# Wide projections with tokens on partitions, and small products issued by chunk halves in turn, in a two-layer hybrid decoder trunk

## The chip, the cores and the metric

The kernel runs on one core of a Trainium2 chip (trn2). The metric is the device time of one execution in microseconds, where lower is better. Three runs of the kernel before took 1239.12, 1239.46 and 1240.7 us, so the median is 1239.46 us.

## The reference

The reference computes DEPTH = 2 decoder layers on 256 tokens of 1024 features, in fp32. Cut to what matters here, one layer is:

```python
proj = x @ w_in                      # columns: q/kv ranks, DeltaNet q k v, HGRN2 q f i, output gates, 3 x 1024 branch gates
a = mla_branch(...)                  # 256 x 512, latent attention
b = gated_deltanet_branch(...)       # 256 x 512, chunks of 64 tokens, triangular solve, scan over 4 chunks
c = hgrn2_branch(...)                # 256 x 512, chunks of 64 tokens, scan over 4 chunks
merged = sum(sigmoid(gate_i) * (branch_i @ w_br_i))      # three branches, each projected to 1024
x = layer_norm(alpha * x + merged @ w_out)
x = layer_norm(alpha * x + moe(x))   # top-1 of 4 groups, top-2 of its 8 SwiGLU experts of width 256
```

The w_in, w_br and w_out products are dense: 256 tokens against 1024 or 512 rows. The chunked branches make many small products of 64 tokens by 64 tokens, or 64 by 128, per head (4 heads) and per chunk (4 chunks of 64 tokens).

## The kernel before

**Stages of a layer.** `layer` (L549) runs the mixer stages in a fixed order of code: decay, latent attention, DeltaNet keys, triangular inverse (`dn_inverse`, L775), queries, values, HGRN2 projections (`hg_project`, L929), HGRN2 local attention (`hg_local`, L951), the two scans (`dn_scan` L872, `hg_scan` L1020), the merge of branch a, the output gates (`gates`, L1051), the merge of branches b and c, `project_out` (L1233), and then the mixture of experts (`moe`, L1453). The framework orders each engine's instructions by readiness in a simulated run, with code order as priority, so dense products of later stages fill the gaps of the earlier ones on TensorE; on the chip every engine then runs its own list in order.

**Dense products.** Weights come in chunks of 1 MB (256 columns by 1024 rows for w_in and w_out; 512 by 512 for the branch projections) into four rotating buffers by DMAs on SP's queue, and from the second half of the mixer on also into 12, then 4 more, prefetch buffers for the experts (`open_prefetch`, L200). Each chunk is split in two pieces of 1024 elements per partition: ScalarE writes the rounded high part `wh` (L225) and VectorE the remainder `wl` (L226; four named pieces go to GpSimd). `mm3` (L234) then makes three fp32r matmuls per 128x128 block: high by high (L237), and the two cross terms (L238, L239). `dense_cm` (L241) holds 128 weight columns stationary and moves 256 tokens, so features land on partitions; `dense_tm` (L252) holds 128 tokens stationary and moves 256 weight columns. Both move 256 columns per matmul. Their results alternate between two PSUM banks, `ps_pa` and `ps_po`: a chunk's 48 matmuls fill one bank, while the other is being read.

**Merge.** For each 256 features of a branch, `merge_branch` (L1213) makes the gate chunk (L1219, `dense_cm`), a tanh by ScalarE (L1221), the branch projection (24 matmuls), the product by VectorE (L1229) and for b and c the addition by GpSimd (L1231) into `mixT`, which has features on partitions. `project_out` splits `mixT` into high and low parts (L1237) and multiplies with w_out in four chunks; after each, `route` (L1243) transposes the new residual and feeds the router product (L1254).

**Small products.** They are plain fp32, each shown as two matmul instructions. `key_products` (L763) and `pairs` (L980) hold 64 tokens (64 output partitions, K = 128): all heads of chunk half 0, then all of half 1. `prod` (L791) and `flip` (L798, L800) in `dn_inverse` work on 64x64 blocks (K = 64, 64 output partitions), half 0 first, then half 1; `flip` uses transposes for half 0 and products with the identity for half 1. `hg_scan` issues, per chunk and head, the product with the state (L1032, K = 128) and the local product (L1033, K = 64) by turns, and after them the state's update (L1038, K = 64, 128 output partitions).

## Time and profile before

| | |
|---|---|
| median of 3 runs | 1239.46 us (1239.12 to 1240.7) |
| the profiled execution | 1233.71 us, span 1231.9 us |
| PE (TensorE matmul) busy | 1090.1 us, 88% |
| PEld (weight load) busy | 842.8 us, 68% |
| DVE / ACT / POOL busy | 639.2 / 439.9 / 181.4 us |
| granted TensorE clock, mean | 0.953 |
| bytes moved | 305.68 MB, mean 248 GB/s |

A matmul's row shows its whole passage through the array, so consecutive matmuls overlap and a busy PE is not a PE at its peak: the distance from one start to the next is the cost of a matmul in a stream, and a merged row of n matmuls spans n - 1 distances plus one passage. A wait that is shorter than a passage doesn't show as idle time.

### The profile page before, as it was taken

Reading aid. Unit: us, or ns where it says so; the run is one execution under the profiler, and the core shown is the slowest. Engines: PE = TensorE matmul, PEld = TensorE weight load, DVE = VectorE, ACT = ScalarE, POOL = GpSimd, SP = SyncE. Lnnn points to the kernel's source line nnn. Section 1 sums busy time; section 2 is a strip of 40 time slices with the busy share of each in tenths; the row PEclk is TensorE's granted clock in tenths of the full one; section 3 lists DMA queues with packets and bytes.
Section 4 is the critical chain, followed back from the end, with each engine's and each line's share of the span. In section 5 each row is a group of like instructions: output and inputs, shape, how many; then the busy total and the mean of one; then the engine's idle time right before and its main releaser. Section 6 shows DMA issues by size and latency. Waiting matters only on the chain. (4 is left out here: it accounts for less than half of the span.)

```text
span 1231.9 us, 23305 instructions
## 1 busy us (share of the span) xinstructions
PE 1090.1 (88%) x9772; PEld 842.8 (68%) x9772; DVE 639.2 (52%) x1320; ACT 439.9 (36%) x812; POOL 181.4 (15%) x168
## 2 busy tenths in 40 slices
PE   6999999999998998777789999899999988977774
PEld 4788987899995644333378889869999944533332
DVE  7775766376567522111086766844766592311113
ACT  4654553354444211000067436535443341100001
POOL 2400033000111400000023010610011141000001
PEclk9999999999999999788899999999999999978887
DMA  8721340358966699999993214205598559999995
GB/s 222 212 70 36 115 150 11 103 172 280 388 247 247 267 419 421 420 422 420 397 243 112 69 37 142 99 1 172 184 355 355 200 228 421 420 422 421 421 420 185
DMA packets 127817, 305.68 MB, mean 248 GB/s; under 512 B 21027, under 2 KB 93149, under 8 KB 102365
## 3 DMA queue, kind: packets, MB, share of 16 engines
q1 hardware_dynamic: 127708, 304.15, 66.6%
q8 instruction: 78, 1.28, 0.4%
q14 instruction: 31, 0.25, 0.1%
HBM read 303.08 MB, written 1.05 MB: 247 GB/s over the span
## 5 line engine op out<-in xcount | busy, mean ns | idle before, releaser
L226 DVE TENSOR_TENSOR wl<-w,wh 128x1024 fp32r<-128x1024 f32 x150 | 203.5, 1358 | 108.3 <-ACT wh L225 108.1
L1550 PE MATMUL ps_pa<-w,xg 128*32 128x256 f32 x2304 | 193.1, 450 | 75.0 <-DMA w<-in_exp_w_up_dram 40.7
L225 ACT CAST wh<-w 128x1024 fp32r<-128x1024 f32 x158 | 165.3, 1047 | 205.5 <-PE ps_pa L238 84.4
L1550 PEld LDWEIGHTS ps_pa<-w,xg 128*32 128x32 f32 x2304 | 89.6, 128 | 174.9 <-DMA w<-in_exp_w_up_dram 54.0
L1557 DVE SCALAR_TENSOR_TENSOR hm<-ps_pa,ws,hm 128x256 f32<-128x256 f32 x18 | 8.7, 484 | 229.8 <-ACT hm L1556 229.8
L237 PE MATMUL ps_pa<-hTh,wh 128*128 128x256 f32 (+1 forms) x360 | 103.3, 287 | 1.9 <-ACT wh L626 1.9
L239 PE MATMUL ps_po<-hTh,wl 128*128 128x256 f32 (+1 forms) x360 | 103.8, 288 | 1.2 <-DVE wl L226 1.2
L239 PE MATMUL ps_pa<-hTh,wl 128*128 128x256 f32 (+1 forms) x360 | 103.2, 287 | 1.5 <-DVE wl L226 1.3
L237 PE MATMUL ps_po<-hTh,wh 128*128 128x256 f32 (+1 forms) x360 | 103.9, 289 | 0.0
L238 PE MATMUL ps_pa<-hTl,wh 128*128 128x256 f32 (+1 forms) x360 | 102.7, 285 | 0.0
L238 PE MATMUL ps_po<-hTl,wh 128*128 128x256 f32 (+1 forms) x360 | 102.5, 285 | 0.0
L1556 ACT ACTIVATE hm<-ps_pa 128x256 f32<-128x256 f32 x18 | 6.9, 384 | 254.1 <-PE ps_pa L1550 254.1
L1576 PE MATMUL ps_pm<-w,hmT 128*32 128x512 f32 x576 | 79.4, 597 | 4.4 <-ACT xg L1504 2.8
L239 PEld LDWEIGHTS ps_pa<-hTh,wl 128*128 128x128 f32 (+1 forms) x360 | 67.4, 187 | 3.7 <-DVE wl L226 2.7
L237 PEld LDWEIGHTS ps_pa<-hTh,wh 128*128 128x128 f32 (+1 forms) x360 | 67.6, 188 | 3.3 <-ACT wh L626 2.1
L239 PEld LDWEIGHTS ps_po<-hTh,wl 128*128 128x128 f32 (+1 forms) x360 | 67.2, 187 | 3.3 <-DVE wl L226 2.7
L237 PEld LDWEIGHTS ps_po<-hTh,wh 128*128 128x128 f32 (+1 forms) x360 | 67.6, 188 | 1.6 <-issue 0.9
L238 PEld LDWEIGHTS ps_po<-hTl,wh 128*128 128x128 f32 (+1 forms) x360 | 67.5, 187 | 0.8 <-issue 0.2
L238 PEld LDWEIGHTS ps_pa<-hTl,wh 128*128 128x128 f32 (+1 forms) x360 | 67.4, 187 | 0.5
L231 DVE TENSOR_TENSOR Yl<-ps_pm,Yh 128x512 fp32r<-128x512 f32 x36 | 24.8, 690 | 72.2 <-ACT Yh L230 65.1
L1576 PEld LDWEIGHTS ps_pm<-w,hmT 128*32 128x32 f32 x576 | 21.0, 109 | 51.0 <-issue 34.7
L226 POOL TENSOR_TENSOR wl<-w,wh 128x1024 fp32r<-128x1024 f32 x8 | 19.5, 2448 | 189.1 <-ACT wh L225 189.1
(486 smaller groups left out, 2460.9 us busy)
## 6 DMA issues: line engine op xcount, KB each, us to landing
w<-in_exp_w_gate_dram SPq DMA_DIRECT2D x66, 1024.0 KB
w<-in_exp_w_up_dram SPq DMA_DIRECT2D x66, 1024.0 KB
w<-in_exp_w_down_dram SPq DMA_DIRECT2D x66, 1024.0 KB
w<-in_w_in_dram SPq DMA_DIRECT2D x58, 1024.0 KB
w<-in_w_out_dram SPq DMA_DIRECT2D x8, 1024.0 KB
w<-in_w_br_a_dram SPq DMA_DIRECT2D x4, 1024.0 KB
w<-in_w_br_b_dram SPq DMA_DIRECT2D x4, 1024.0 KB
w<-in_w_br_c_dram SPq DMA_DIRECT2D x4, 1024.0 KB
```

The costliest lines, as they stand in the source:

```text
L225: nc.scalar.copy(v(hi), raw)
L226: engine.tensor_tensor(v(lo), raw, v(hi).bitcast(F32), op=OP.subtract)
L231: (engine or self.nc.vector).tensor_tensor(lo, src, hi.bitcast(F32), op=OP.subtract)
L237: mm(ps, a[0], b[0], start=start, stop=False, skip_group_check=True)
L238: mm(ps, a[0], b[1], start=False, stop=False, skip_group_check=True)
L239: mm(ps, a[1], b[0], start=False, stop=stop, skip_group_check=True)
L1550: nc.tensor.matmul(pg[32 * e:32 * e + 32, FF * n:FF * n + FF], xgs[gp, k // 4][j][:, k % 4, 32 * e:32 * e + 32], w[:, FF * k:FF * k + FF], ...
L1556: nc.scalar.activation(hm, pg[:, 0:FF], AF.Silu)
L1557: self.last_hm = nc.vector.scalar_tensor_tensor(hm, pg[:, FF:2 * FF], PTs[gp][1][:, j], hm, op0=OP.mult, op1=OP.mult).ins
L1576: nc.tensor.matmul(ps[32 * e:32 * e + 32], hmT[:, i, 32 * e:32 * e + 32], w[:, D * i + 512 * c:D * i + 512 * c + 512], start=(i == 0), sto ...
```

## The change

- The columns of HGRN2's i, of the two output gates, of the three branch gates and of w_out come in chunks of 512 columns by 512 rows (two chunks make one output of 512 features). They and the branch projections go through a new `dense_tm`: 128 tokens stationary, 512 weight columns moving, so that tokens lie on partitions. One output of 512 features now fills both banks, one per token block of 128, and each piece is used first for block 0 (6 matmuls), then for block 1 (6).
- `merge_branch` works on 512 features at a time, with two tanh, two products and two additions into `mix` (tokens on partitions).
- `mix` is transposed on TensorE (`mix_turned`) in two halves: the first before the last branch projection, the second after the first half of w_out's first output. The split into high and low reads PSUM then.
- `project_out` makes two outputs of 512 features; `route` works per token block and 512 features.
- `key_products`, `prod`, `flip` and `pairs` issue the two chunk halves in turn, head by head; `flip` uses products with the identity for both.
- `hg_scan` issues the state's updates of both halves in turn, then all local products of both halves in turn, and then those with the state.
- The pool `sg` has 4 buffers where it had 3.

The core of the diff:

```diff
-    def dense_tm(self, ps, raw, act, name):
-
-        nk = raw.shape[1]
-        for k0 in range(0, nk, 4):
-            w = self.split(raw[:, k0:k0 + 4], f"{name}.{k0 // 4}")
+    def dense_tm(self, ps, raw, act, name, k0, nk):
+
+
+        for j in range(0, 4, 2):
+            w = self.split(raw[:, j:j + 2], f"{name}.{j // 2}")
             for t in range(TB):
-                for k in range(4):
-                    self.mm3(ps[t], [x[:, k0 + k, 128 * t:128 * t + 128] for x in act], [x[:, k] for x in w],
-                             k0 + k + t == 0, k0 + k == nk - 1)
+                for k in range(2):
+                    kk = k0 + j + k
+                    self.mm3(ps[t], [x[:, kk, 128 * t:128 * t + 128] for x in act], [x[:, k] for x in w],
+                             kk == 0, kk == nk - 1)
+
+    def wide(self, l, n, act):
+
+        ps = [self.ps("pa") for _ in range(TB)]
+        for i in range(2):
+            self.wide_half(ps, l, n, act, i)
+        return ps
...
+            def between():
+                xp.close()
+                pool = po.enter_context(tc.tile_pool(name=f"out{l}", bufs=1, **side))
+                self.mixS = [pool.tile([128, 8, T], F32R, name=n) for n in ("mixh", "mixl")]
+                self.mix_turned(0)
...
         def prod(ps, lhs, rhs, t):
             pv = ps[:, 0:256].rearrange("p (a i) -> p a i", i=C)
-            for c in range(2):
-                r = slice(64 * c, 64 * c + 64)
-                for h in range(NH):
+            for h in range(NH):
+                for r in (slice(0, 64), slice(64, 128)):
                     nc.tensor.matmul(pv[r, h], lhs[r, 4 * t + h], rhs[r, 4 * t + h], start=True, stop=True)
...
             for h in range(NH):
-                nc.tensor.transpose(pv[0:64, h], x[0:64, 4 * t + h], eye[0:64])
-            for h in range(NH):
-                nc.tensor.matmul(pv[64:128, h], x[64:128, 4 * t + h], eye[64:128], start=True, stop=True)
+                for r in (slice(0, 64), slice(64, 128)):
+                    nc.tensor.matmul(pv[r, h], x[r, 4 * t + h], eye[r], start=True, stop=True)
...
         for n in range(4):
             t, c = divmod(n, 2)
-            r = slice(64 * c, 64 * c + 64)
-            po = self.ps()
-            for h in range(NH):
-                oo = po[r, 128 * h:128 * h + 128]
-                if S is not None:
-                    nc.tensor.matmul(oo, self.hqd[:, h, 64 * n:64 * n + 64], S[:, h], start=True, stop=False)
-                nc.tensor.matmul(oo, self.hatt[r, 4 * t + h], self.hv[r, t, h], start=(S is None), stop=True)
+            r = half[c]
+            if c == 0:
+
+                po, pk = self.ps(), [self.ps() for i in range(2) if n + i < 3]
+                for h in range(NH):
+                    for i, p in enumerate(pk):
+                        nc.tensor.matmul(p[:, 128 * h:128 * h + 128], self.hkd[half[i], 4 * t + h], self.hv[half[i], t, h],
+                                         start=True, stop=True)
+                for h in range(NH):
+                    for q in half:
+                        nc.tensor.matmul(po[q, 128 * h:128 * h + 128], self.hatt[q, 4 * t + h], self.hv[q, t, h],
+                                         start=(h == 0), stop=False, skip_group_check=True)
+            if S is not None:
+                for h in range(NH):
+                    nc.tensor.matmul(po[r, 128 * h:128 * h + 128], self.hqd[:, h, 64 * n:64 * n + 64], S[:, h],
+                                     start=False, stop=True, skip_group_check=True)
             nc.scalar.copy(o[r, t].rearrange("p h e -> p (h e)"), po[r])
...
+        for c in range(2):
+            sg = [self.gp.tile([128, 512], F32, name="sg", tag="sg", bufs=self.NB["sg"]) for _ in range(TB)]
+            for s, ps in zip(sg, self.wide(l, f"gl{br}{c}", self.hT)):
+                nc.scalar.activation(s, ps, AF.Tanh, scale=0.5)
+            if c and between:
+                between()
+            n = f"br_{br}{c}"
+            ps = [self.ps("pa") for _ in range(TB)]
+            self.dense_tm(ps, self.w(l, n).rearrange("p (k c) -> p k c", k=4), oT, n, 0, 4)
+            self.done(l, n)
+            for t in range(TB):
+                mv = self.mix[:, t, 512 * c:512 * c + 512]
+                nc.vector.scalar_tensor_tensor(mv if br == "a" else sg[t], sg[t], 1.0, ps[t], op0=OP.add, op1=OP.mult)
+                if br != "a":
+                    nc.gpsimd.tensor_tensor(mv, mv, sg[t], op=OP.add)
+
+    def mix_turned(self, c):
+
+        for k in range(4 * c, 4 * c + 4, 2):
+            ps = self.ps()
+            for kk in range(2):
+                for t in range(TB):
+                    self.nc.tensor.transpose(ps[:, 256 * kk + 128 * t:256 * kk + 128 * t + 128],
+                                             self.mix[:, t, 128 * (k + kk):128 * (k + kk) + 128], self.ident)
+            self.split_act(*[x[:, k:k + 2].rearrange("p k t -> p (k t)") for x in self.mixS], ps)
...
+        for c in range(2):
+            ps = [self.ps("pa") for _ in range(TB)]
+            for i in range(2):
+                self.wide_half(ps, l, f"wo{c}", self.mixS, i)
+                if c == 0 and i == 0:
+                    self.mix_turned(1)
+                if c == 1 and i == 0:
+                    for t in range(TB):
+                        route(t, 0)
```

## Rows read from the trace of the kernel before

**Rows 1.** Chain that ended last, its final DMA: start us, us, what

```profile
1192.23 19.71 DMA w<-in_exp_w_down_dram
```

**Rows 2.** Windows: stretch, length, busy time (instructions) per engine, PEclk, DMA share, GB/s

```profile
60.00:160.00 100.00, 100.00 (x1057) 90.47 (x1056) 70.48 (x160) 52.80 (x122) 7.98 (x9) 1.00 0.27 80
160.00:202.00 42.00, 37.19 (x399) 35.28 (x398) 31.02 (x32) 20.10 (x22) 20.08 (x13) 0.92 0.28 91
202.00:231.00 29.00, 28.91 (x197) 19.92 (x197) 11.30 (x14) 8.43 (x12) 3.10 (x3) 1.00 0.01 1
...
440.00:600.00 160.00, 123.62 (x1141) 61.01 (x1133) 27.65 (x65) 16.95 (x38) 2.23 (x6) 0.89 1.01 421
```

**Rows 3.** Timeline of PE in the inverse: start us, us, line, tile, shapes, count

```profile
82.69 0.96 PE L791 MATMUL ps_pb<-d,d 64*64 64x64 f32 x16
...
86.60 0.41 PE L798 MATMUL ps_pb<-mconst,d 64*64 64x64 f32 x4
86.94 0.50 PE L800 MATMUL ps_pb<-mconst,d 64*64 64x64 f32 x5
...
87.33 0.22 PE L791 MATMUL ps_pb<-d,d 64*64 64x64 f32 x1
87.34 0.22 PE L800 MATMUL ps_pb<-mconst,d 64*64 64x64 f32 x1
87.39 0.22 PE L791 MATMUL ps_pb<-d,d 64*64 64x64 f32 x1
```

**Rows 4.** Timeline of PE: attention's output by turns, key products, local pairs

```profile
56.21 0.66 PE L1205 MATMUL ps_pm<-a,a 128*64 128x128 f32 x8
...
73.43 0.97 PE L763 MATMUL ps_pb<-d 128*64 128x64 f32 x16
...
172.07 1.90 PE L980 MATMUL ps_pm<-a,a 128*64 128x64 f32 x32
```

**Rows 5.** Timeline of DVE at the end of the local stage, with the wait before it

```profile
199.18 0.75 DVE L982 COPY_PREDICATED a<-mconst,ps_pm 128x512 f32<-128x512 int32 x1 [1.41 <-PE ps_pm L980]
```

**Rows 6.** Timeline of PE in the second step of the HGRN2 scan

```profile
213.01 0.43 PE L1032 MATMUL ps_pm<-a,a 128*64 128x128 f32 x2
213.37 0.43 PE L1033 MATMUL ps_pm<-a,a 64*64 64x128 f32 x2
213.73 0.93 PE L1038 MATMUL ps_pm<-a,a 64*128 64x128 f32 x6
```

**Rows 7.** Timeline of PE: a gate chunk's first and 48th matmul, and matmuls of 512 columns

```profile
239.35 0.29 PE L237 MATMUL ps_po<-hTh,wh 128*128 128x256 f32 x1
...
244.99 0.28 PE L239 MATMUL ps_po<-hTh,wl 128*128 128x256 f32 x1
...
447.84 0.39 PE L1589 MATMUL ps_sum<-Yh,PT 128*128 128x512 f32 x1
448.07 0.39 PE L1589 MATMUL ps_sum<-Yl,PT 128*128 128x512 f32 x1
...
395.65 0.81 PE L326 MATMUL ps_pa<-bits 128*128 128x512 bf16 x3
```

**Rows 8.** Timelines of ACT, DVE and PE around one chunk pair of branch b

```profile
299.13 1.05 ACT L225 CAST wh<-w 128x1024 fp32r<-128x1024 f32 x1 [2.27 <-PE ps_po L238]
300.08 0.59 ACT L1221 ACTIVATE sg<-ps_po 128x512 f32<-128x512 f32 x1
...
300.21 1.23 DVE L226 TENSOR_TENSOR wl<-w,wh 128x1024 fp32r<-128x1024 f32 x1 [2.10 <-ACT wh L225]
302.20 0.69 DVE L1229 SCALAR_TENSOR_TENSOR sg<-sg,ps_pa 128x512 f32<-128x512 f32 x1 [0.77 <-PE ps_pa L239]
303.09 2.25 DVE L226 TENSOR_TENSOR wl<-w,wh 128x1024 fp32r<-128x1024 f32 x1 [0.20 <-ACT wh L225]
...
305.39 0.38 PE L239 MATMUL ps_po<-hTh,wl 128*128 128x256 f32 x1 [0.19 <-DVE wl L226]
```

**Rows 9.** Timeline of PE: eight fp32 transposes of 128x128

```profile
202.41 1.03 PE L1012 MATMUL ps_pm<-const,a 128*128 128x128 f32 x8
```

More of the change, by code (lines that the diff above doesn't have):

```diff
@@ L31, with both @@
 CH = {"cq": (0, 256), "ckv": (256, 160), "ba": (1952, 128)}
-for _n, _c in (("dn_q", 416), ("dn_k", 928), ("dn_v", 1440), ("dn_gate", 1960), ("hg_q", 2472), ("hg_f", 2984),
-               ("hg_i", 3496), ("hg_gate", 4008), ("gla", 4520), ("glb", 5544), ("glc", 6568)):
-    for _i in range(4 if _n[:2] == "gl" else 2):
+for _n, _c in (("dn_q", 416), ("dn_k", 928), ("dn_v", 1440), ("hg_q", 2472), ("hg_f", 2984)):
+    for _i in range(2):
         CH[f"{_n}{_i}"] = (_c + 256 * _i, 256)
+WIDE = {"hg_i": ("w_in", 3496), "dn_gate": ("w_in", 1960), "hg_gate": ("w_in", 4008)}
+for _b, _c in (("gla", 4520), ("glb", 5544), ("glc", 6568), ("wo", 0)):
+    for _i in range(2):
+        WIDE[f"{_b}{_i}"] = ("w_out" if _b == "wo" else "w_in", _c + 512 * _i)
+def both(n):
+    return [f"{n}0", f"{n}1"]
 def merge_order(b):
-    return [f"gl{b}0", f"br_{b}0", f"gl{b}1", f"gl{b}2", f"br_{b}1", f"gl{b}3"]
+    return both(f"gl{b}0") + [f"br_{b}0"] + both(f"gl{b}1") + [f"br_{b}1"]
 ORDER = ["cq", "ba", "ckv", "dn_k0", "dn_k1", "dn_q0", "dn_q1", "dn_v0", "dn_v1",
@@ L44 @@
     ["dn_gate0", "dn_gate1", "hg_gate0", "hg_gate1"] + merge_order("b") + merge_order("c") + \
-    ["wo0", "wo1", "wo2", "wo3"]
+    both("wo0") + both("wo1")
 EXPERT = ("exp_w_gate", "exp_w_up", "exp_w_down")
@@ L579, in layer @@
                 self.router_weights(l)
[L580 removed]
+                self.mix = self.gp.tile([128, TB, D], F32, name="mix")
                 self.pq = self.ps("pm")
@@ L603, in layer @@
             self.merge_branch(l, "b")
-            self.merge_branch(l, "c")
-            xp.close()
-            with tc.tile_pool(name=f"out{l}", bufs=1, **side) as po:
+            po = ExitStack()
+            def between():
[3 more added lines that the diff above has]
+                self.mix_turned(0)
+            self.merge_branch(l, "c", between)
+            with po:
                 self.project_out(l, po)
@@ L787, in prod @@
             pv = ps[:, 0:256].rearrange("p (a i) -> p a i", i=C)
-            for c in range(2):
-                r = slice(64 * c, 64 * c + 64)
-                for h in range(NH):
+            for h in range(NH):
+                for r in (slice(0, 64), slice(64, 128)):
                     nc.tensor.matmul(pv[r, h], lhs[r, 4 * t + h], rhs[r, 4 * t + h], start=True, stop=True)
@@ L941, in rows512 @@
     def rows512(self, l, n, dst, silu2=False):
-        for c in range(2):
-            ps = self.ps("pa")
-            pv = ps.rearrange("p (t c) -> p t c", t=TB)
-            self.dense_tm([pv[:, t] for t in range(TB)], self.wcols(l, f"{n}{c}"), self.hT, f"{n}{c}")
-            self.done(l, f"{n}{c}")
-            d, pv = dst[:, :, 2 * c:2 * c + 2], pv.rearrange("p t (h e) -> p t h e", h=2)
+        for t, ps in enumerate(self.wide(l, n, self.hT)):
+            d, pv = dst[:, t], ps.rearrange("p (h e) -> p h e", h=NH)
             self.later(self.silu2(d, pv, d) if silu2 else self.nc.scalar.copy(d, pv))
@@ L1234, in project_out, with route @@
         nc, A = self.nc, self.A
-        mixS = [po.tile([128, 8, T], F32R, name=n) for n in ("mixh", "mixl")]
-        for c in range(0, 8, 2):
-            self.split_act(*[x[:, c:c + 2] for x in mixS], self.mixT[:, c:c + 2], self.nc.gpsimd if c == 2 else None)
-        r, st = self.h, self.stats(4)
+        r, st = self.h, self.stats(2)
         pr = self.ps()
-        def route(c):
+        def route(t, c):
             ps = self.ps()
-            for t in range(TB):
-                for kk in range(2):
-                    k = 2 * c + kk
-                    nc.tensor.transpose(ps[:, 256 * kk + 128 * t:256 * kk + 128 * t + 128], r[:, t, 128 * k:128 * k + 128],
-                                        self.ident)
-            x = self.gp.tile([128, 2, T], F32, name="sg", tag="sg", bufs=self.NB["sg"])
-            for kk in range(2):
-                nc.scalar.copy(x[:, kk], ps[:, 256 * kk:256 * kk + 256])
-            for kk in range(2):
-                nc.tensor.matmul(pr[0:36, 0:T], self.rw[:, 2 * c + kk, 0:36], x[:, kk], start=(c + kk == 0), stop=(c + kk == 4))
@@ new lines, in route @@
+            x = self.gp.tile([128, 4, 128], F32, name="sg", tag="sg", bufs=self.NB["sg"])
+            nc.scalar.copy(x.rearrange("p k t -> p (k t)"), ps)
+            for k in range(4):
+                nc.tensor.matmul(pr[0:36, 128 * t:128 * t + 128], self.rw[:, 4 * c + k, 0:36], x[:, k],
+                                 start=(t + c + k == 0), stop=(c + k == 4), skip_group_check=True)
+        for c in range(2):
+            ps = [self.ps("pa") for _ in range(TB)]
[4 more added lines that the diff above has]
+                if c == 1 and i == 0:
+                    for t in range(TB):
+                        route(t, 0)
+            cs = slice(512 * c, 512 * c + 512)
+            for t in range(TB):
+                nc.vector.scalar_tensor_tensor(r[:, t, cs], self.h[:, t, cs], 2 * ALPHA, ps[t], op0=OP.mult, op1=OP.add)
@@ L1270, in project_out @@
                 nc.vector.bn_stats(st[:, t, c], r[:, t, cs])
-            self.done(l, f"wo{c}")
-            if c:
-                route(c - 1)
-        route(3)
+        for t in range(TB):
+            route(t, 1)
         self.logits = pr[0:36, 0:T]
```

63 lines of the change are left out of this document (18 added, 45 removed).

## The prediction

> **What bounds the kernel now.** I read the chain of waits first. It ends in experts' weights: the last transfer before the final products alone holds the chain for 19.7 us [rows 1], and the reader sees nothing else in the last 200 us. The windows by stage tell how far that reaches [rows 2]. From 440 to 600 us the DMA share is 1.01 at 421 GB/s, and PE has a lower clock (0.89) because it waits: the expert stage lasts as long as its bytes. It begins with full prefetch buffers, so a mixer that ends earlier moves the stage as a whole; a microsecond saved in the mixer is a microsecond saved in the total. In the mixer DMA is at 0.01 to 0.28 of its time in the three stretches up to 231 us, and PE is busy for 100.00 of 100.00 us from 60 to 160 and for 28.91 of 29.00 from 202 to 231: there the order of the work is a PE queue that never runs dry. Between them, 160 to 202, PE is busy for 37.19 of 42.00 and the granted clock is 0.92: the local stage of HGRN2 waits for VectorE and GpSimd (31.02 and 20.08 us busy). After 231 us it is dense products to about 386 us. The second layer repeats these stretches within 5 us.
>
> Then I read starts on PE, since passages overlap. One layer is worked out; both count.
>
> **A. Products of 64x64 by turns (inverse, keys).** Sixteen matmuls of one `prod` span 0.96 us, of which 0.22 is the last one's passage: (0.96 - 0.22) / 15 = 0.049 us apart, 0.79 us for the sixteen [rows 3]. Where a flip's second half (lower right block of the array) meets the next product's first half (upper left), their starts are 0.01 us apart and the pair repeats after 0.06 us [rows 3]: two blocks run side by side, 0.03 us per matmul. In the order before, that happens only at the seam. By turns it would hold throughout: 16 x 0.029 = 0.46, a saving of 0.33 us for each of 20 products: 6.6 us. A flip is 4 transposes in 86.94 - 86.60 = 0.34 us and 8 matmuls at about 0.056, 0.80 together [rows 3]; as 16 matmuls by turns 0.46: 10 x 0.34 = 3.4 us. Bounds: nothing, if the array already overlaps what it can, to 10 us.
>
> The key products hold K = 128 and alternate in columns only. The nearest row is attention's output, which already goes by column halves: (0.66 - 0.27) / 7 = 0.055 apart (0.27 us being the passage of one of them) with 128 columns in two passes, half of what such a matmul takes alone in the scan's rows below [rows 4, 6]. The key products stand at (0.97 - 0.22) / 15 = 0.050 [rows 4]; I take 0.040, between 0.028 and no change: 4 x 16 x 0.010 = 0.6 us. A is 10.6 us. The inverse is also a chain through VectorE, and the order was planned without knowing of the overlap, so some of it will turn into waits: I take 9.0.
>
> By the Trainium skill (TensorE: Matmul & The Clock Gate, Part 3, what overlaps and what doesn't) a weight load overlaps running matmuls only where the row groups differ. By that rule column halves of K = 128 gain nothing, A would lose 0.6 us and B its whole gain; the row of attention's output, by column halves at half the lone distance, speaks against it [rows 4].
>
> **B. Local pairs.** 32 matmuls take 1.90 us, (1.90 - 0.22) / 31 = 0.054 apart [rows 4]; at 0.040 a call falls to 1.28, seven calls save 4.3 us of PE. But here PE is not the bound. What counts is where VectorE waits for the pairs, 1.41 us at the end of the stage [rows 5]. I take 1.5 us, between 0 and 3.
>
> **C. HGRN2 scan.** L1032 and L1033, which differ in K, come by turns, and each pair takes 0.36 us from start to start, 0.18 per matmul; L1038, of one kind in a row, (0.93 - 0.27) / 5 = 0.13 and less [rows 6]. The 0.07 in between is the change of shape. Before: 3 steps x 8 x 0.36 = 8.7, the first step 0.9, updates 3 x 8 x 0.115 = 2.8, together 12.4 us. After: updates and local products by halves in turn at 0.055 (as [rows 4]): 16 + 32 matmuls, 2.6; one lone update 0.9; three state products of 8 at 0.115, 2.8: 6.3 us. Saved 6.1. DeltaNet's scan beside it keeps its shape changes and is a chain of its own of some 23 us in this window of 29; gate chunks of branch a fill. I take 5.0, between 2 and 6.1.
>
> **D. Wide dense products.** A gate chunk's 48 matmuls start from 239.35 to 244.99: 5.64 / 47 = 0.120 us for 256 columns. The only stream of 512 columns in this number format repeats after 0.23 us [rows 7]. So a wide one saves 2 x 0.120 - 0.231 = 0.009. Outputs that have tokens stationary already lose no turn of the operands, and for them I take half of that, 0.004, between nothing and 0.009. Per layer 432 of the first kind (18 chunks' worth) and 240 of the second: 3.9 + 1.0 = **4.9** us saved.
> Remainders: with GpSimd adding, one remainder takes 2.25 instead of 1.23 us and PE gets it 0.45 late [rows 8]; that happens 7 times in branches b and c. Wide, the additions come in pairs behind a split that has more room; I take 4 times 0.15: **2.6** saved (0 to 3).
> Hand-over of the banks, a new wait: an output fills both banks, so block 0's bank has to be read in the 6 x 0.231 = 1.39 us before block 1 ends. After a branch projection the reader is VectorE: the next piece's cast is released when the last piece but one ends, 0.2 + 1.05 + 0.08 later the remainder begins and lasts 1.23 [rows 8], so the product (0.69) starts at 2.55 and ends at 3.24, and PE, which wants the bank at 2.77, stands 0.5 us. Six times: 3.0. Behind it on VectorE are the next remainder, and PE for that. The two gates need ACT 0.59 and DVE 0.69 in a row: 1.0 each. w_out's first output 0.5, HGRN2's i 0.3. Together **5.8** lost (0 if the readers slip in early, up to 16).
> Transposes: 16 new ones, 8 in a row took 1.03 us [rows 9], in four groups with a change of kind each 0.45: **1.8** lost. The split work on ACT and DVE is the same as before, only from PSUM.
> The second half of `mix`: after the last branch projection come two products, two additions of about 1.3 us, transposes, cast and remainder; w_out's first half covers 5.5 us of that, but the transposes stand behind it in the code, and the cast and remainder (0.6 + 0.7) are bare: **1.3** lost; the start of `project_out` has waits of this kind now, about **1.2**, which go.
> SP issues the same number of weight transfers, each with longer rows; the router's products and the tail after w_out cost what they did (the last residual block and its statistics are as late as before). D: 4.9 + 2.6 - 5.8 - 1.8 - 1.3 + 1.2 = -0.2, between -10 and +8.
>
> **Sum.** 9.0 + 1.5 + 5.0 - 0.2 = 15.3 us per layer, 30.6 in all. The profiled execution took 1233.7 us (its span and 1.8 around it) and would take 1203; the median of the runs stands 5.8 above it, and from it 1239.5 - 30.6 = **1209 us**.
>
> **Rivals.**
> *Hidden gain.* The inverse and the pairs may be paced by their chains through VectorE (70.48 of 100.00 us busy [rows 2]), or the blocks do not run side by side when each matmul brings its own weights. For it: waits shorter than a passage don't show. Against it: the seam in [rows 3]. Only part of C is left, 2.0 - 0.2 per layer: 1239.5 - 3.6 = 1236.
> *Wide streams at full pace.* Three bf16 matmuls of 512 columns repeat after (0.81 - 0.39) / 2 = 0.21 us [rows 7]. If a long fp32r stream does too, 672 x 0.021 = 14 us more per layer: 1209 - 28 = 1181. Against it: every pair of L1589 stands at 0.23. The Trainium skill's figure in the same page (Back-to-back issue gap) is 512 / 2.4 + 2.5 = 216 ns, which would be an estimate of 10 us per layer.
> *Column halves gain nothing* (the rule on row groups above): 2 x (0.6 + 1.5) less, 1213, inside the forecast's own range.
> *Slower: the banks' hand-over.* Place: the first matmul of each of 17 outputs per layer. If the planner puts the reader of block 0 behind the next pieces' work, PE waits 2.5 us after each branch projection (a stretched remainder 2.25 and the product), 1.2 after each gate chunk, 3 at the output gates and 2 at the other three: 15 + 7 + 6 + 6 = 34 us for 5.8, which is 28 per layer worse: 1209 + 56 = 1265. It decides the sign from 5.8 + 15.3 = 21 us per layer, 1.2 us per output. For it: in [rows 8] the tanh stands behind a cast that serves a later piece, at 0.95 us. Against it: with weights moving, the piece's buffer is freed by the same matmul as the bank, and the reader comes first in code order.
>
> **How the numbers follow.** Forecast (1195 to 1225) 0.55, column rule 0.05 within it in time, wide streams 0.10, hidden gain 0.17, slower 0.13. A measurement of this kernel tells about 0.2%, 2.5 us. Of the hidden gain's 0.17 a little over half lies below 1237: faster 0.55 + 0.05 + 0.10 + 0.10 = 0.80, same 0.07, slower 0.13. For the range, 8 in 10: from the upper bounds of A to C with D a little above nothing (10.6 + 3 + 6.1 + 6 = 26 per layer, 1239.5 - 52 = 1187) to the hidden gain at 1236; the slower case and most of full pace are left out.
>
> **What would show it.** Right: `prod` of sixteen spans about 0.65 us instead of 0.96, the scan window shrinks by some 5 us, the wide matmuls stand 0.23 apart, gaps of 0.5 us before the first matmul behind each branch projection, the expert stage as long as now. Wrong: `prod` unchanged, or PE idle in the inverse behind VectorE; gaps over 1.2 us at most outputs; an expert stage that starts earlier but ends at the same time.

## The result and the profile after

The changed kernel takes 1212.5 us (median of four runs, 1212.31 to 1213.93) against 1240.1 for the kernel before on the same chip: a ratio of 0.978, with a 95% interval of 0.976 to 0.980. That is 27.6 us less, where 30.6 were forecast. Here and below, an execution that took over 1.5% longer than the fastest of its kernel is left out of ratios, intervals and spreads; that happened to two executions of the scan alone. The profiled execution has a span of 1210.5 us, 21.4 less than before's 1231.9. The difference of 6 us lies in the profile before, not in the change: it was an execution 6 us below the median of its kernel, and further down TensorE's clock offers a reason.

Windows of the changed kernel: the same stretches as [rows 2], the last one 20 us earlier.

```profile
60.00:160.00 100.00, 98.48 (x1140) 88.58 (x1140) 72.35 (x166) 55.47 (x126) 7.73 (x9) 1.00 0.31 94
160.00:202.00 42.00, 36.65 (x351) 26.95 (x349) 28.79 (x32) 20.57 (x23) 22.22 (x14) 0.92 0.21 69
202.00:231.00 29.00, 28.07 (x174) 20.71 (x174) 14.04 (x16) 11.25 (x16) 3.13 (x2) 1.00 0.24 74
420.00:580.00 160.00, 124.08 (x1165) 63.00 (x1153) 30.36 (x71) 18.18 (x40) 3.71 (x10) 0.88 1.01 419
```

The expert stage is what it was: DMA at 1.01, and 202.3 and 202.7 us from the first to the last `up` product in the two layers, 202.1 and 201.9 before. So it did move as a whole, and the gain was made in the mixer, as forecast. In the mixer the inverse is now not quite dense (98.48 of 100.00 us), which is new.

Timeline of PE in the changed kernel: a `prod` (now L818), a `flip` (L826), local pairs (L1002), and of the HGRN2 scan the local products (L1060) and those with the state (L1064).

```profile
83.18 0.68 PE L818 MATMUL ps_pb<-d,d 64*64 64x64 f32 x16 [1.04 <-DVE small L292]
87.39 0.68 PE L826 MATMUL ps_pb<-mconst,d 64*64 64x64 f32 x16
200.85 1.15 PE L1002 MATMUL ps_pm<-a 128*64 128x64 f32 x32 [0.86 <-DVE a L1020]
206.53 1.09 PE L1060 MATMUL ps_pm<-a,a 64*64 64x128 f32 x16
211.40 1.09 PE L1064 MATMUL ps_pm<-a,a 128*64 128x128 f32 x8
```

`prod` spans 0.68 us where it spanned 0.96 [rows 3]: (0.68 - 0.22) / 15 = 0.031 us from start to start, so two blocks run side by side throughout. The pairs, which alternate in columns only, fell from 1.90 [rows 4] to 1.15: (1.15 - 0.22) / 31 = 0.030 apart. The local products of the scan stand at (1.09 - 0.27) / 15 = 0.055, those with the state at 0.117.

Timeline of all engines in the changed kernel (its DVE and PE lines) behind a branch projection of b.

```profile
287.88 0.68 DVE L1259 SCALAR_TENSOR_TENSOR sg<-sg,ps_po 128x512 f32<-128x512 f32 x1
...
288.14 0.40 PE L248 MATMUL ps_pa<-wh,o 128*128 128x512 f32 x1
...
288.71 0.47 PE L246 MATMUL ps_po<-wh,hTh 128*128 128x512 f32 x1 [0.17 <-DVE sg L1259]
...
289.02 0.39 PE L247 MATMUL ps_po<-wl,hTh 128*128 128x512 f32 x1
...
289.25 0.39 PE L248 MATMUL ps_po<-wh,hTl 128*128 128x512 f32 x1
```

This is the hand-over of a bank: VectorE reads block 0's bank until 288.56, and the next output starts at 288.71, 0.57 us behind the matmul before it; the one after it comes 0.31 later, and then the pace is 0.23. That is 0.42 us lost, where 0.5 was forecast.

Timeline of PE in `project_out` of the changed kernel, around the transposes of the second half of `mix` (L1269).

```profile
347.16 0.39 PE L248 MATMUL ps_pa<-wh,mixl 128*128 128x512 f32 x1
347.39 0.60 PE L1269 MATMUL ps_pb<-const,mix 128*128 128x128 f32 x4
347.83 0.60 PE L1269 MATMUL ps_pm<-const,mix 128*128 128x128 f32 x4
349.18 0.50 PE L246 MATMUL ps_po<-wh,mixh 128*128 128x512 f32 x1 [0.75 <-ACT mixh L239]
...
350.55 0.50 PE L248 MATMUL ps_po<-wh,mixl 128*128 128x512 f32 x1 [0.18 <-DVE mixl L240]
```

The transposes end, and then PE waits for ScalarE's cast (0.75 us behind its last passage) and for VectorE's remainder (0.18): the bare work that was forecast at 1.3 us.

Timeline of DVE in the changed kernel where the local stage of HGRN2 begins: the logarithm's sum (L986), DeltaNet's state (L934) and HGRN2's prefix sums (L989).

```profile
173.43 1.23 DVE L986 TENSOR_TENSOR a<-a,a 128x1024 f32<-128x1024 f32 x1
177.66 0.69 DVE L934 TENSOR_TENSOR d<-d,ps_pb 128x512 f32<-128x512 f32 x1 [3.01 <-PE ps_pb L927]
178.26 2.43 DVE L989 TENSOR_TENSOR_SCAN a<-scanm,a 128x256 f32<-128x256 f32 x4
```

Here is something that no step of the prediction had: most of DeltaNet's scan now runs inside HGRN2's local stage (it ends 8.6 us behind the last local pair, 22.9 before), and its update stands ahead of HGRN2's prefix sums on VectorE and waits 3.01 us for PE. The prefix sums, ready at 174.7, start at 178.26. In layer 0 the last product of the inverse ends 7.8 us earlier than before, the last local pairs 0.1 us later, and DeltaNet's scan 14.2 us earlier. HGRN2's scan takes 13.9 us from its first product to the end of its last, where it took 28.0.

To see what is lost and what is only moved, the mixer is cut at three points that every kernel has: the first `flip`, VectorE's first clamp of the forget gates (the head of the local stage) and the first matmul of the output gates. The windows of the middle stretch, clamp to gates, in both layers, before (columns as in [rows 2]):

```profile
165.71:256.63 90.92, 86.01 (x758) 74.95 (x758) 50.54 (x53) 37.76 (x52) 23.18 (x16) 0.96 0.27 83
...
770.83:858.73 87.90, 83.72 (x758) 72.49 (x757) 51.31 (x53) 37.75 (x52) 24.61 (x16) 1.00 0.27 87
```

And of the changed kernel:

```profile
164.24:245.12 80.88, 74.33 (x561) 55.18 (x560) 47.32 (x53) 39.16 (x65) 25.36 (x16) 0.96 0.27 86
...
756.40:837.31 80.91, 74.20 (x561) 55.08 (x560) 47.34 (x53) 39.17 (x65) 25.18 (x16) 0.96 0.27 86
```

The third column from the right is the granted clock. In the execution before, layer 1 kept 1.00 and took 87.90 us, layer 0 had 0.96 and took 90.92. Other executions of the kernel before have lower mean clocks (down to 0.944, against 0.953 here) and take up to 1241 us. So the clock is the likely reason why the profile before lies under its median; no profile of a slower execution of it was taken.

### The profile page after: what moved, and what is told of

The parts are those of the page before. It is cut to its first block, busy times and chain, and to the rows that moved or that the text cites. A ratio compares the mean times of both kernels' runs of the same rounds, so it can differ in the third digit from the quotient of the medians.

```text
span 1210.5 us, 20874 instructions
## 1 busy us (share of the span) xinstructions
PE 1063.3 (88%) x8572; PEld 754.2 (62%) x8572; DVE 603.5 (50%) x1306; ACT 441.8 (36%) x804; POOL 188.4 (16%) x166
## 5 line engine op out<-in xcount | busy, mean ns | idle before, releaser
L246 PE MATMUL ps_po<-wh,hTh 128*128 128x512 f32 x144 | 58.3, 405 | 1.0 <-DVE mix L1259 0.5
L246 PE MATMUL ps_pa<-wh,hTh 128*128 128x512 f32 x144 | 58.2, 404 | 1.1 <-DVE mix L1259 0.6
L247 PE MATMUL ps_pa<-wl,hTh 128*128 128x512 f32 x144 | 58.3, 405 | 0.9 <-POOL wl L235 0.6
L247 PE MATMUL ps_po<-wl,hTh 128*128 128x512 f32 x144 | 58.3, 405 | 0.9 <-POOL wl L235 0.6
L248 PE MATMUL ps_pa<-wh,hTl 128*128 128x512 f32 x144 | 57.9, 402 | 0.0
L248 PE MATMUL ps_po<-wh,hTl 128*128 128x512 f32 x144 | 57.9, 402 | 0.0
L1606 PEld LDWEIGHTS ps_pm<-w,hmT 128*32 128x32 f32 x576 | 21.9, 109 | 47.2 <-issue 32.9
L246 PE MATMUL ps_pa<-hTh,wh 128*128 128x256 f32 (+1 forms) x168 | 49.2, 293 | 1.9 <-ACT wh L654 1.9
L248 PE MATMUL ps_pa<-hTh,wl 128*128 128x256 f32 (+1 forms) x168 | 49.1, 292 | 0.7 <-DVE wl L235 0.5
L248 PE MATMUL ps_po<-hTh,wl 128*128 128x256 f32 (+1 forms) x168 | 49.1, 292 | 0.5 <-DVE wl L235 0.5
L246 PE MATMUL ps_po<-hTh,wh 128*128 128x256 f32 (+1 forms) x168 | 49.1, 293 | 0.0
```

What stands on the lines that cost most here:

```text
L246: mm(ps, a[0], b[0], start=start, stop=False, skip_group_check=True)
L247: mm(ps, a[0], b[1], start=False, stop=False, skip_group_check=True)
L248: mm(ps, a[1], b[0], start=False, stop=stop, skip_group_check=True)
L1606: nc.tensor.matmul(ps[32 * e:32 * e + 32], hmT[:, i, 32 * e:32 * e + 32], w[:, D * i + 512 * c:D * i + 512 * c + 512], start=(i == 0), sto ...
```

## The experiments

All ratios are to the kernel before, run on the same chip; the gain is (1 - ratio) x 1239.46 us. The lengths are those of the three stretches of one profiled execution (first flip to clamp, clamp to gates in layers 0 and 1, gates to the last router product); "clock" is the granted clock of the middle one.

| kernel | ratio (95%) | gain | flip to clamp | clamp to gates | clock | gates to router |
|---|---|---|---|---|---|---|
| before | 1 | | 86.8 | 90.9, 87.9 | 0.96, 1.00 | 131.0 |
| small | 0.986 (0.984-0.988) | 17.6 | 80.7 | 87.5, 90.5 | 0.98, 0.92 | 131.2 |
| scan | 1.000 (0.997-1.003) | 0.0 | 86.8 | 92.3, 90.9 | 0.91, 0.92 | 131.1 |
| wide | 1.000 (0.999-1.002) | -0.4 | 90.7 | 87.7, 88.3 | 1.00, 0.98 | 129.6 |
| small + scan | 0.986 (0.984-0.988) | 17.1 | 80.7 | 84.2, 93.3 | 0.96, 0.87 | 131.1 |
| small + wide | 0.989 (0.988-0.991) | 13.3 | 84.7 | 86.5, 86.5 | 0.94, 0.96 | 129.7 |
| scan + wide | 0.992 (0.990-0.993) | 10.3 | 90.7 | 82.0, 82.6 | 1.00, 0.98 | 129.6 |
| all: the change | 0.978 (0.976-0.980) | 27.1 | 84.7 | 80.9, 80.9 | 0.96, 0.96 | 129.7 |
| the change, pairs as before | 0.982 (0.979-0.984) | 22.8 | 84.6 | 82.0, 82.6 | 1.00, 0.98 | 129.7 |

### The small products alone

The kernel before with the change's `key_products`, `prod`, `flip` and `pairs`:

```diff
-            for c in range(2):
-                r = slice(64 * c, 64 * c + 64)
-                for h in range(NH):
+            for h in range(NH):
+                for r in (slice(0, 64), slice(64, 128)):
                     nc.tensor.matmul(pv[r, h], lhs[r, 4 * t + h], rhs[r, 4 * t + h], start=True, stop=True)
...
```

> The kernel before with key_products, prod, flip and pairs by chunk halves in turn; the scan and the dense products as before. The forecast's terms A and B: 2 x (9.0 + 1.5) = 21 us, 1240.1 - 21 = 1219. Rival 1 (the local stage is paced by VectorE and GpSimd, so only what the inverse itself gained stays): 2 x 8.5 = 17 us, 1223. Rival 2 (the local stage gives back what the inverse gains, as the trace of after seems to show: last product 7.8 us earlier, last pairs 0.1 us later): under 4 us, 1236 or more. All agree that prod spans 0.68 us.

Measured: 1221.8 us, 17.6 less by the ratio. This is nearer the first rival's 1223 than the forecast's 1219, but the runs (1219.9 to 1223.6) cannot tell the two apart. To the end of the last inverse product 8.4 us per layer are won, at the clamp 6.1 are left, and PE stands for 1.5 us in that stretch (80.71 us, 79.22 busy), where it stood for none.

### The scan alone

The kernel before with only `hg_scan` reordered:

```diff
+                for h in range(NH):
+                    for i, p in enumerate(pk):
+                        nc.tensor.matmul(p[:, 128 * h:128 * h + 128], self.hkd[half[i], 4 * t + h], ...)
+                for h in range(NH):
+                    for q in half:
+                        nc.tensor.matmul(po[q, 128 * h:128 * h + 128], self.hatt[q, 4 * t + h], ...)
...
```

> The kernel before with only hg_scan reordered (updates by halves in turn, local products by halves in turn, then the state products). The forecast's term C: 2 x 5.0 = 10 us, 1230. Rival 1 (DeltaNet's scan of some 23 us beside it bounds the window): 2 x 2 = 4 us or less, 1236. Rival 2 (the scan's order carries the 14 us per layer by which the scan window of after is shorter): 2 x 14 = 28 us, 1212.

Measured: no gain (median 1239.6 us; ratio 1.000, interval 0.997 to 1.003), against the forecast's 10 us. But the runs spread widely: nine took 1227.65 to 1245.61 us, and they follow the mean granted clock of the run. The shortest had 0.952, the next two 0.946 (1232.17) and 0.943 (1236.55), the four longest 0.934 to 0.937. Two runs of the kernel before with 0.952 took 1233.6 and 1235.9 us, so at the same clock the reordered scan is 6 to 8 us faster; that is read off a single run of the scan alone. The windows of its profiled execution, clamp to gates:

```profile
166.95:259.24 92.29, 86.37 (x758) 77.71 (x757) 50.63 (x53) 37.74 (x52) 22.68 (x16) 0.91 0.26 82
...
773.43:864.29 90.86, 84.95 (x757) 76.69 (x757) 51.33 (x53) 37.73 (x52) 23.12 (x16) 0.92 0.26 84
```

A clock of 0.91 over 92.29 us is 8.3 us of full clock lost. Taken off the busy time, it leaves 86.37 - 8.3 = 78.1 us of work, and 77.7 in layer 1. The same sum for before is 86.01 - 0.04 x 90.92 = 82.4 and 83.7. So by this estimate, which takes PE as busy wherever the clock was low, 4 to 6 us of work per layer did go, and the clock took them back.

### The wide dense products alone

The changed kernel with all small products and `hg_scan` put back, so that the wide outputs and the transposed `mix` are left. The core of what it keeps:

```diff
-            self.chunk_cm(ps, l, f"gl{br}{c}")
+            for s, ps in zip(sg, self.wide(l, f"gl{br}{c}", self.hT)):
...
```

> The changed kernel with key_products, prod, flip, pairs and hg_scan put back: the wide dense products and the transposed mix alone. The forecast's term D: -0.2 per layer, 1240.1 + 0.4, no change that can be told. Rival 1 (the wide order also lets the planner place the scans earlier): 5 to 10 us faster, 1230 to 1235. Rival 2 (D costs what the local stage lost in the trace of after, some 8 us per layer): 1256.

Measured: 1239.6 us, ratio 1.000 (0.999 to 1.002). The forecast's -0.2 per layer holds, and both rivals (1230 to 1235, 1256) fall. It is a sum of parts, though: the head of the mixer is 3.9 us longer (the wide product for HGRN2's i falls into it), gates to router 1.4 us shorter, and the clock of the middle stretch is 1.00 and 0.98. It is also the wide order that moves DeltaNet's scan: here too it ends 8.3 us behind the last local pair, 22.9 before.

### Small products and scan

The first two edits together on the kernel before:

```diff
+                for r in (slice(0, 64), slice(64, 128)):
...
+        half = (slice(0, 64), slice(64, 128))
...
```

> The kernel before with all small products and hg_scan as in the changed kernel, dense products and mix as before. The forecast: 2 x 15.5 = 31 us, 1209, at or a little below the changed kernel (1212.5). If the wide products carry a gain of their own, this stays above 1212.5 by that gain; if they cost (the gates lost about 3 us per layer in the trace of after, the merges gained about 3), it lies below by that cost. The parts add up if the sum of the gains of the runs with the small products alone and with the scan alone is this one's within 4 us.

Measured: 1222.2 us where 1209 was forecast, no better than the small products alone; the parts do add up (17.6 + 0.0), but 10 us are missing to the changed kernel. Where they are shows in layer 1, in windows of 5 us:

```profile
780.00:785.00 5.00, 2.75 (x61) 2.53 (x63) 5.00 (x6) 2.96 (x3) 3.61 (x2) 1.00 0.00 0
785.00:790.00 5.00, 3.61 (x37) 2.58 (x33) 4.96 (x6) 3.90 (x5) 0.00 (x0) 1.00 0.01 3
790.00:795.00 5.00, 5.00 (x31) 4.11 (x32) 1.94 (x3) 0.58 (x1) 0.00 (x0) 0.57 0.00 0
795.00:800.00 5.00, 5.00 (x28) 3.96 (x28) 1.50 (x3) 0.00 (x0) 3.09 (x3) 0.50 0.00 0
800.00:805.00 5.00, 5.00 (x19) 3.06 (x18) 0.00 (x0) 0.58 (x1) 0.00 (x0) 0.50 0.00 0
805.00:810.00 5.00, 5.00 (x23) 4.22 (x22) 1.39 (x3) 0.58 (x1) 0.00 (x0) 0.50 0.00 2
```

PE is busy for only 2.75 and 3.61 of 5 us at the end of the local stage, where it waits for VectorE; then the granted clock falls to 0.50, the lower level (1.2 GHz), and stays there for the scans, in which PE is the bound (5.00 of 5.00 busy). In layer 0 the clock of the middle stretch is 0.96 and it takes 84.2 us; in layer 1 it is 0.87 and it takes 93.3, by the same instructions. What the clock costs them shows in the timeline of PE, with the same products of DeltaNet's scan in layer 0, at a clock of 1.00, and in layer 1, at 0.50:

```profile
206.75 1.16 PE L899 MATMUL ps_pb<-d,d 64*128 64x128 f32 x8
...
803.37 2.07 PE L899 MATMUL ps_pb<-d,d 64*128 64x128 f32 x8
```

From the end of the last local pair to the end of HGRN2's scan, layer 0 takes 23.3 us where the small products alone take 29.8: at full clock the scan's order is worth 6.5 us there, without the wide products. Layer 1 takes 32.9 us, where the small products alone take 29.5.

### Small products and wide products

The changed kernel with `hg_scan` put back as it was before:

```diff
-        half = (slice(0, 64), slice(64, 128))
...
+            for h in range(NH):
+                oo = po[r, 128 * h:128 * h + 128]
...
```

> The changed kernel with only hg_scan put back. So far: small products alone 17 to 18 us faster, scan alone and wide products alone nothing, small products and scan 17 us, all three 27.6 us. Theory 1 (the scan's order is worth its 5 us per layer only where TensorE's granted clock stays at 1.0 in the scan window, which the wide order gives it; in the run of small products and scan it stood at 0.50 to 0.57 from 790 to 810 us): here the 10 us of the scan are missing, 1212.5 + 10 = 1222. Theory 2 (the missing 10 us come from small and wide products together, the scan's order gives nothing): 1212 to 1214.

Measured: 1225.2 us, ratio 0.989 (0.988 to 0.991). The first theory's number holds, and is passed by 3 us: beside small and wide products the scan's order is worth 27.1 - 13.3 = 13.8 us by the ratios, each of which is good to some 2 us. From clamp to gates it is 86.5 - 80.9 = 5.6 us per layer, at a clock that is alike in the two (0.94 and 0.96 against 0.96). The clock of 1.0 that the theory asked for is found in neither.

### Scan and wide products

The changed kernel with the small products put back:

```diff
-            for h in range(NH):
-                for r in (slice(0, 64), slice(64, 128)):
+            for c in range(2):
+                r = slice(64 * c, 64 * c + 64)
+                for h in range(NH):
...
```

> The changed kernel with the small products put back. Theory 1 (the scan's order gains where wide products keep the clock up): 1240 - 10 = 1230. Theory 2 (the 10 us need small and wide products together): 1240.

Measured: 1228.8 us, ratio 0.992 (0.990 to 0.993). The first theory holds again: beside wide products the scan's order is worth 10.3 + 0.4 = 10.7 us, 5.4 per layer. The first and the last products of HGRN2's scan in layer 0, by the timelines of PE, with the wide products alone:

```profile
210.96 1.08 PE L1057 MATMUL ps_pm<-a,a 64*64 64x128 f32 x8
...
231.52 0.43 PE L1057 MATMUL ps_pm<-a,a 64*64 64x128 f32 x2
```

and with scan and wide products:

```profile
210.27 0.94 PE L1058 MATMUL ps_pm<-a,a 64*128 64x128 f32 x12 [0.28 <-ACT a L1037]
...
223.00 1.09 PE L1066 MATMUL ps_pm<-a,a 128*64 128x128 f32 x8
```

That is 21.0 us against 13.8. The windows of this kernel, clamp to gates:

```profile
169.46:251.43 81.97, 76.94 (x565) 58.45 (x564) 47.48 (x53) 39.09 (x65) 25.33 (x16) 1.00 0.26 84
...
770.88:853.43 82.55, 78.32 (x565) 59.93 (x564) 48.07 (x53) 39.08 (x65) 24.92 (x16) 0.98 0.26 84
```

With the wide order the clock stays at 1.00 and 0.98, where the scan alone had 0.91 and 0.92, and the scan's gain is kept. Why the wide order keeps it up was not tried by itself: PE stands nearly as long (81.97 - 76.94 = 5.0 and 4.2 us, 5.9 in the scan alone), only at other places, and DeltaNet's scan lies elsewhere too.

### Products of constants in the local stage

Small products and scan, with the local stage filled:

```diff
             ps = self.ps()
+            for _ in range(8):
+                nc.tensor.matmul(ps, self.bits[:, 0], self.bits[:, 0:1].to_broadcast([128, 4, 128]), start=True, stop=True)
```

> The run of small products and scan (1222), with 8 products of constants (128x512 in bf16, some 0.21 us each) ahead of each of the seven local pairs, which overwrite their result: the work is the same, and TensorE stands less in the local stage. Theory 1 (the granted clock that falls behind the local stage's waits takes the scan's gain): the clock of the scan window stays at 1.0 in both layers and the time falls to 1213 to 1218. Rival (the scan window is bound by DeltaNet's chain, the clock costs nothing): no fall; up to 2 x 7 x 8 x 0.21 = 24 us slower where the added products stand in the way.

Measured: 1233.9 us, 11.7 us more than without them (medians), so they cost half of their 24 us. From clamp to gates layer 0, whose clock was 0.96 and stays 0.96, grew from 84.2 to 94.1; layer 1, whose clock rose from 0.87 to 0.96, only from 93.3 to 95.3. The difference, 7.9 us, is what the clock gave back where it rose. As a remedy the filling is worthless: in layer 0 the added products raise PE's busy time by 12.0 us, and the time for which it stands falls only from 7.1 to 5.0. The rival, that the clock costs nothing, falls; the first theory's number is missed.

### HGRN2's i behind the local stage

```diff
-        self.rows512(l, "hg_i", v)
         self.hq, self.hv = q, v
+
+    def hg_values(self, l, mp):
+        self.rows512(l, "hg_i", self.hv)
...
-                      "dn_values hg_forget hg_project hg_local dn_scan hg_scan"
+                      "dn_values hg_forget hg_project hg_local hg_values dn_scan hg_scan"
```

> The changed kernel with the product for HGRN2's i moved in code from ahead of the local stage to behind it; nothing else changes. Theory 1 (in the changed kernel this wide product, 48 x 0.234 = 11 us, stands ahead of the local chain, which begins 6 us later against the last inverse product than before and then leaves TensorE idle): it fills the gaps of the local stage, up to 8 us per layer, 1197 to 1206. Theory 2 (the end of the scans is set by DeltaNet's chain, or by the sum of TensorE's work): 1210 to 1214.

Measured: 1218.5 us, 6 us slower than the changed kernel. The local stage does begin earlier (flip to clamp 69.1 us instead of 84.7) and in layer 0 its last pairs end 21 us earlier, but clamp to gates takes 100.5 and 99.0 us instead of 80.9. The sum is 2.5 to 4 us longer: PE's work was moved, not removed, PE stands for 7.6 and 7.5 us instead of 6.5 and 6.7, and the clock of the stretch is 0.93 and 0.95. Neither theory's range holds the time; the first had the sign wrong. The late local stage of the changed kernel is no loss: what fills the time ahead of it is work that has to be done.

### The pairs put back

The changed kernel with the order of `pairs` from before:

```diff
-            for t in range(TB):
-                for h in range(NH):
-                    for c in range(2):
-                        o = 128 * t + 64 * c
+            for c in range(2):
+                for t in range(TB):
+                    o = 128 * t + 64 * c
+                    for h in range(NH):
```

> The changed kernel with only the local pairs put back (all heads of half 0, then of half 1). The forecast's term B: 1.5 us per layer, 1212.5 + 3 = 1215.5. Theory 1 (the local stage is paced by VectorE and GpSimd; in the changed kernel TensorE stands there for 6 us per layer, so a pair that is 0.75 us shorter only makes it stand longer): 1212.5, within 2 us. Theory 2 (the longer pairs keep TensorE's clock up, the changed kernel loses 3.4 us per layer of clock there): 1208 to 1212.

Measured: 1215.4 us, ratio 0.982 against 0.978; the two intervals overlap, but the stretches are clear: clamp to gates grows from 80.9 to 82.0 and 82.6. The pairs are worth 1.1 and 1.7 us per layer, as forecast (1.5), and 2.9 us in all by the medians. They take 7 x 0.75 = 5.3 us of PE's time away; of that PE stands 1.5 to 2.2 us more, and the clock falls from 1.00 and 0.98 to 0.96, which is 3.2 and 1.6 us. So of theory 2 the sign of the clock's share is right, and the time is not.

### Other banks

```diff
-        ps = [self.ps("pa") for _ in range(TB)]
+        ps = [self.ps(tag) for _ in range(TB)]
...
-            ps = [self.ps("pa") for _ in range(TB)]
+            ps = [self.ps("pa" if br == "a" else None) for _ in range(TB)]
...
-            ps = [self.ps("pa") for _ in range(TB)]
+            ps = [self.ps(None if c else "pa") for _ in range(TB)]
```

(`tag` is `None`, the banks of the small products, for the second output gate.)

> The changed kernel with other PSUM banks (of the two pools that the small products have left by then) for the branch projections of b and c, the second output gate and the second half of w_out, so that no output has to wait for the reader of the one before. The forecast's hand-over term: 0.5 us behind each of four branch projections and 1.0 at an output gate, 0.5 at w_out, 3 to 3.5 us per layer: 1206. Rival (the next remainder on VectorE is as late as the reader was, so PE stands at the next piece instead): 1211 to 1212.5.

Measured: 1208.5 us, ratio 0.976 (0.974 to 0.978). Gates to router shrinks from 129.7 to 127.5 us, 2.2 per layer, where the forecast's term said 3 to 3.5. The timeline of PE behind the same branch projection:

```profile
287.68 0.39 PE L248 MATMUL ps_pb<-wh,o 128*128 128x512 f32 x1
287.91 0.40 PE L246 MATMUL ps_po<-wh,hTh 128*128 128x512 f32 x1
```

The 0.57 has become 0.23, and the products that follow keep that pace: nothing else takes the wait's place here, and the rival falls. Of the 2.2 us the merges hold 1.2, w_out 0.7 and the gates 0.3. The hand-over at the gates, forecast at 1.0 each, was all but free.

### w_out by halves

```diff
-        for c in range(2):
-            ps = [self.ps("pa") for _ in range(TB)]
-            for i in range(2):
-                self.wide_half(ps, l, f"wo{c}", self.mixS, i)
+        ps = [[self.ps(None if c else "pa") for _ in range(TB)] for c in range(2)]
+        for i in range(2):
+            for c in range(2):
+                self.wide_half(ps[c], l, f"wo{c}", self.mixS, i)
...
```

The second half of `mix` is turned behind the first quarter, the router's first products come behind the third.

> The changed kernel with w_out's two outputs by halves: first halves of both, with the second half of the mix transposed and split between them, then the second halves of both. The forecast's term for the second half of the mix (1.3 us bare) and w_out's hand-over (0.5) go: 1.8 per layer, 1209. Rival (the router's products, now behind the third quarter, come later and lengthen the tail by as much): 1212 to 1215.

Measured: 1209.8 us, ratio 0.977 (0.975 to 0.980). Gates to router shrinks to 127.7, 2.0 per layer, all in w_out. The tail did not grow (4.8 us from the last product of w_out to the router's end in both), so the rival falls.

### Both

The two edits above together:

```diff
+        ps = [[self.ps(None if c else "pa") for _ in range(TB)] for c in range(2)]
...
+            ps = [self.ps("pa" if br == "a" else None) for _ in range(TB)]
...
```

> Both of the last two edits on the changed kernel: other banks for the branch projections of b and c and the second output gate, and w_out's two outputs by halves (in banks of both kinds). From the stretch between the first product of the branch gates and the router, which each shortened by 2.0 to 2.2 us per layer: 2 x 4.2 = 8.4 us if they add up, 1212.5 - 8.4 = 1204. Rival (both remove the same waits, those around w_out): 1207 to 1208.

Measured: 1206.7 us, ratio 0.975 (0.972 to 0.977), the best of all. Gates to router is 126.0 us, 3.7 per layer less than in the changed kernel; the two edits share 0.5 us, all of it inside w_out, so they don't add up fully, and the time comes nearer the rival's 1207 than to 1204. The window of layer 1:

```profile
834.18:960.20 126.02, 124.02 (x562) 97.95 (x562) 75.09 (x126) 55.25 (x73) 16.55 (x9) 1.00 0.73 271
```

## Why the prediction was right, and which steps were not

The time came within 3.5 us of the forecast, inside its range, and its main mechanism, matmuls on two blocks of the array side by side, is what the rows show. By steps, per layer:

**A, the inverse (9.0).** Right in mechanism, and a little high: 8.4 us to the end of the last inverse product. At the clamp 6.1 are left; PE now stands for 1.5 us there, the waits for which 1.6 had been taken off.

**B, the pairs (1.5).** Right in time, 1.1 and 1.7, and for the reason given: PE is not the bound. The starts are closer than the 0.040 assumed (0.030), so column halves of K = 128 overlap as the row halves do. By the rule of the Trainium skill (TensorE: Matmul & The Clock Gate, Part 3) that a weight load overlaps running matmuls only in other row groups, read as the prediction read it, the pairs would still take 1.90 us; they take 1.15, so that rival falls.

**C, the HGRN2 scan (5.0).** Right in size where the clock holds. Beside the wide products it is 5.4 to 5.6 per layer by the stretches (up to 6.9 by the ratios), out of 7.2 by which HGRN2's scan itself shrinks (21.0 to 13.8); without them it is nothing in the time, though 6.5 in the one layer whose scans ran at 1.00. The step that failed is "I take 5.0", in a window for which the prediction read a clock of 1.00 [rows 2] and took that as given. The clock belongs to the kernel: in the scan alone, and in layer 1 of small products and scan, PE lost it in a stretch where the kernel before had 0.96 or 1.00, and that cost as much as the order brought. In small products and scan the fall to 0.50 behind 790 us stands behind waits for VectorE and ScalarE, of 1.69 us at most between 780 and 790 us. The Trainium skill (TensorE: Matmul & The Clock Gate, HAM oscillation) tells of a clock that falls behind waits for DMA; the rows agree in that the fall stands behind waits, and show no more of it. The sign "the scan window shrinks by some 5 us" was passed by far, 28.0 to 13.9; with the wide products alone, which move DeltaNet's scan, it is already 21.0.

**D, the wide products (-0.2).** Right as a sum: 0.4 us lost in all, by the interval between 1.1 won and 2.0 lost. Streams: 0.234 us for 512 columns, forecast 0.231; the rival of full pace (0.21) falls. Merges of b and c (to the end of VectorE's last product) from 71.9 to 68.8 us, 3.1 less; forecast 2.6 of streams and 2.6 of remainders, less four hand-overs (2.0) and half of the transposes (0.9), 2.3. w_out with the router's products from 30.4 to 32.3, 1.9 more; forecast 1.1. These two misses cancel. The term that was wrong is the gates' hand-over, "1.0 each": gates and their transposes take 28.6 us where they took 28.8, against 1.6 more forecast.

**The sum.** The prediction added its terms as if they were independent; 17.6 + 0.0 - 0.4 is 17.2, and the change brought 27.1. Beside the wide products the small ones are worth 13.3 + 0.4 = 13.7 us and the scan's order, added last, 13.8, where 21 and 10 were forecast. That the sum came so near is in part luck: the one fell short and the other ran over.

**Where the 3 us went.** From the first flip to the gates the terms A, B and C made 15.5 us per layer; in layer 0, where the clock of the middle stretch was 0.96 before and after, 177.7 became 165.6, 12.1. PE stands 1.5 us more ahead of the clamp and 1.6 more behind it (6.5 against 4.9). From the gates on the forecast was 0.4 longer and it became 1.3 shorter. In layer 0 that leaves 3.4 - 1.7 = 1.7 us short. The books don't close over the whole execution, though. In layer 1, where the execution before kept a clock of 1.00, the same stretch gives only 9.3 us (174.7 to 165.3); outside the stretches, ahead of the first flip, between the layers and at the end, the changed execution is 2.8 us longer; and the profile before lies 6 us under its median. How these share the 3.0 us by which the gain fell short stays open.

The slower rival (banks' hand-over) had the right place and the wrong size: 0.42 us behind a branch projection, far from the 1.2 per output that would have decided the sign, and 2.2 us per layer in all by the run with other banks. Hidden gain falls with the inverse.

## What to carry to other kernels

Issue small matmuls so that neighbours use different blocks of the array, by rows or by columns; here that cost nothing but the order of the code and was worth 17.6 us alone and 13.7 beside the wide products. When a kernel's stages alternate between a chain on other engines and a stretch that TensorE bounds, read the granted clock of the second stretch in every variant, and time edits together as well as alone: an edit that shows nothing by itself may be worth 5 us per layer next to another, as the scan's order was here. When outputs become as large as all the banks they rotate through, give their next user banks that have gone idle; that was worth 2.2 us per layer here.

## What the hardware showed that was not expected

The same program, with the scan alone reordered, ran from 1227.65 to 1245.61 us as its mean granted clock went from 0.952 to 0.936, while the kernel before stayed within 1233.6 to 1241.2. In small products and scan the clock stood at 0.50 (1.2 GHz) through 15 us in which PE was busy without a break (795 to 810 us above), behind two windows with 2.75 and 3.61 of 5 us busy. In the changed kernel 2.04 of 5 us were busy from 780 to 785, and the clock was 0.74 there, 0.58 in the next 5 us and then 1.00. What makes the difference was not found. An addition by GpSimd took 1.79 us on average, in pairs, where it took 1.34 in single ones: the first of a pair took about 1.3 us, the second, which ran beside a remainder on VectorE, about 2.3.
